# A hybrid attention / RWKV step on one core: per-head means in one fp32 product, key and query loads over 128 partitions, RWKV's room released in two steps

## The chip, the cores and the metric

The kernel runs on one core of one Trainium2 chip. The metric is the device time of one launch in microseconds (us); lower is better. The kernel before took 2118.08, 2123.41 and 2121.22 us in three runs, a median of 2121.22. The profile is of one more execution, of 2118.56 us, whose span (first to last instruction) is 2116.8 us at a mean granted TensorE clock of 0.98.

## The reference

One step of a two-layer model over 256 context and 1024 latent tokens of width 1024. Layer 0 projects the normed input to attention queries, keys, values and gates and to the operands of a bidirectional RWKV scan, runs both, gates each branch, and projects back. Layer 1 does the same with a chunked gated linear attention (GLA). Cut to what the change touches:

```python
z = h @ w_in
qa, ka, va, ga, zb, gb = split_cols(z, EV_SPLITS)
q = rms_norm(qa.reshape(B, T, H_A, HD_A), qn_g)   # a mean of squares over the 64 columns of each head
k = rms_norm(ka.reshape(B, T, KV_A, HD_A), kn_g)
...                                               # RWKV: kk is normalised per head too
o_a = block_attention(q, keys, vals) * jax.nn.silu(ga)      # 8 query heads, 2 key heads, 64 wide, fp32
```

## The kernel before, in words

**Who sets the order.** The kernel is written as generators that hand every operation to a list scheduler (class `Sched`, L86 on). It estimates a start and a cost for each operation, keeps a time for every engine, and issues the one that can start first; where an operation may go to several engines, `_best` (L271) takes the cheapest by start + cost + a fee of the engine (`WORTH`, L112). So a changed fee or cost moves instructions anywhere in the program. The resulting order on TensorE (PE), VectorE (DVE), ScalarE (ACT) and GpSimd (POOL) is fixed when the kernel is built: each engine runs its list in order and stalls at the first instruction whose input is missing. Transfers are issued by SP, also in order. Each takes one of eight semaphores in turn (DMAHW0 to 7) and is not issued until the transfer eight before it, on the same semaphore, has ended. All recorded instructions carry the line number of the issuing helper (L354), so the profile is read by tile names.

**Layer 0's projections (0 to 525 us).** Weights and activations are split in high and low parts (`hhi`, `hlo`, `whi`, `wlo`; type fp32r), and each product of a projection is three fp32r products (`mm3`), 8 k-slices deep: 24 rows of PE per 128 columns and 512 tokens. Results land in the PSUM tiles `pj`. Queries, keys and RWKV's kk need a mean of squares per head. `head_means` (L965) gets it as a product with the 128x128 block matrix `bones`: it splits the squares into `hi` (a cast) and `lo` (a subtraction) and adds two fp32r products in a PSUM tile `a`.

**The changeover (about 515 to 560 us).** When the projections have let go of their memory, `room_attn` (L1187) lays out attention's tiles and `room_rwkv` (L1248) RWKV's. Keys come from `kh` in DRAM: `KA` holds the high part of a key head in rows 0 to 63 and the low part in rows 64 to 127, `KB` the high part again in rows 0 to 63 and a row of ones (row 64). A query tile `QA` holds the high part of a head's queries twice, `QB` the low part and, in row 64, the negated row maximum `mr`. Loads of `KA` and `QA` are two transfers of 64 partitions each. `maxima` (L1615) makes one product KA,QA per 128 queries and 512 keys and reduces it on DVE (`mx`); `attend` (L1648) then makes the score pair KA,QA and KB,QB, an exponential (`pt`) and the product with the values `VO`. `mod_cols` (L548) computes modulation columns from the weights `mw`.

**RWKV beside attention (560 to 1240 us).** Four head pairs run a chunked scan of small products (`AR`, `BK`, `Vs` are loaded per segment; `Z`, `TT`, `U` and others are its tiles); `rwkv_norm` (L1562) normalises `y` with fp32 products with `bones`. Attention fills in between, in 12 units with two heads each.

**After it.** `room_proj` (L2211) closes RWKV's memory and starts to load layer 0's output weights; the output projection runs at about 1310 to 1450 us, layer 1 to about 1990, its output projection to the end.

Of the kernel before, what the change touches and what calls it, by code (L numbers as in the profile page):

```python
# [20 lines left out]
P = 128  # L21
# [82 lines left out]
class Sched:  # L104
# [4 lines left out]

    OWN = {"dve": 0.085, "act": 0.085}  # L110
    SWITCH = 0.095
    WORTH = {"dve": 0.2, "act": 0.0, "pool": 0.6}  # L112
    AFTER = {"pe": 0.07, "": -0.13}
    UNTIL = {"pe": 0.26, "pool": 0.19, "dve": 0.13, "act": 0.13}

# [60 lines left out]
    def _instr(self, name, op, f, a, k):  # L176
# [19 lines left out]
        if name == "pe":  # L196
            lhs = pattern(k.get("lhsT", a[1] if len(a) > 1 else None))
            m = 1
            for d in lhs.shape[1:]:
                m *= d  # L200
            rows = lhs.shape[0]
            turned = op == "transpose" or k.get("is_transpose")

            if turned:
                cost = max(2 * n / 2300, m / 1170)
            elif lhs.dtype == F32:
                cost = 2 * max(2 * n / 2300, m / 1170)
            elif lhs.dtype == F32R:
                cost = max(n / 2300, m / 1170)
            else:  # L210
                cost = max(n, 64) / 2300
            cost = 1.06 * cost + 0.0025
            size = lambda x: 32 if x <= 32 else 64 if x <= 64 else P
            late = (size(rows), size(m), lhs.start_partition() // 32, out.start_partition() // 32)
        elif name == "dve":
            srcs = [x for _, x in aps if x is not out]
            psum = any(x.tensor.space == PSUM for x in [out] + srcs)
            if op == "reduce_max":
                n = 1
# [12 lines left out]
            late = not psum and op != "reduce_max"  # L232
            if op in ("tensor_scalar", "scalar_tensor_tensor"):
                cost += (0.0, 0.057, 0.09)[sum(1 for x in srcs if x.shape[1:] == [1] or tuple(x.shape[1:]) == (1,))] if n > 1 else 0.0
        elif name == "act":
            psum = any(x.tensor.space == PSUM for _, x in aps)
            cost = (0.051 if psum else 0.094) + n * 0.833e-3
            if n > 1:
                cost += (0.0, 0.05, 0.17)[min(2, sum(1 for q, x in aps if q in ("scale", "bias", 2)))]
            if out.shape[0] <= 64 and n > 1:  # L240
                cost += 0.11
        elif name == "pool":
            if op == "tensor_tensor":
                cost = 0.15 + n * (1.66e-3 if any(0 == d[0] for _, x in aps for d in x.ap[1:]) else 2.1e-3)
                if k.get("op", a[-1]) == ALU.pow:
                    cost = 0.56
            elif op == "memset":
                cost = 0.14 + n * 0.42e-3
            else:
                cost = 0.16 + n * (0.833e-3 if len(aps) == 2 else 1.5e-3)  # L250
            late = op != "memset"
        else:
            cost, late = 0.47, n * out.shape[0] * 4 / 270e3
        return f, a, k, name, cost, late, reads, writes, slots

    def _choice(self, slot, taken=()):
# [14 lines left out]
    def _best(self, ins):  # L271

        if len(ins) == 9:
            return ins
        ts = [(self._start(x), x) for x in ins[9]]
        if ts[0][0] is None:
            return ins[9][0]
        return min(ts, key=lambda x: x[0] + x[1][4] + self.WORTH.get(x[1][3], 0.0)
                   + (self._beside(x[1][3], x[0], x[1][4]) if x[1][3] in self.port and x[1][5] else 0.0))[1]

    def _start(self, ins, spare=0.0):
# [202 lines left out]
def tile_hybrid_dit_step(ctx: ExitStack, tc: tile.TileContext, I, C, O):  # L484
# [63 lines left out]
    def mod_cols(i, c0, n, bank, row, ready=lambda: True):  # L548
# [15 lines left out]
                b = yield from get(row, False)  # L564
                D.dma_start(out=b[0:2, 0:n], in_=I["mod_b"][i:i + 1, c0:c0 + n].to_broadcast([2, n]))
        yield from sch.until(ready)
        for a in range(2):
            with sch.together():
                for s in range(4):
                    k = 4 * a + s  # L570
                    PE.matmul(p[32 * s:32 * s + 32, :], lhsT=sT[:, k, :], rhs=ws[k // nk][:, k % nk, :], start=(a == 0), stop=(a == 1))
            for x in ws[4 * a // nk:4 * (a + 1) // nk]:
                put("mw", x)
        m4 = yield from get("m4", False)
        m = m4[:, 0:n]
        copy(m, p)
# [123 lines left out]
    vt_d = [dram.tile([T, P], F32, name=f"vt{p}") for p in range(4)]  # L700
    bv_d = [dram.tile([P, T], F32, name=f"bv{p}") for p in range(4)]
    kh_d = dram.tile([P, 2, PAST + T], F32, name="kh")
    vo_d = dram.tile([P, 14, P], F32, name="vo")
    ga_d = [dram.tile([P, T], F32, name=f"ga{p}") for p in range(4)]
    gb_d = [dram.tile([P, T], F32, name=f"gb{p}") for p in range(4)]
# [6 lines left out]

    get, put = sch.get, sch.put
    el = cst.tile([P, 2, 4, 20], F32, name="el")
    left, right = (ctx.enter_context(ExitStack()) for i in range(2))
    flags = dict(left=0, gates=0, attn=False, keys=False, rwkv=False, mods=False, normed=False, gla=False, gl=False, units=0)

    def pool(stack, name, **k):
        return stack.enter_context(tc.tile_pool(name=name, bufs=1, reuse_waits="tile", **k))
# [18 lines left out]
    def layer0():  # L738
# [44 lines left out]

        def gated(col, dst):

            def use(g, t0, n, p):
                t1 = yield from get("gt", False)
                S.activation(out=t1[:, 0:n], in_=p, func=AF.Tanh, scale=0.5)
                V.scalar_tensor_tensor(out=t1[:, 0:n], in0=t1[:, 0:n], scalar=1.0, in1=p, op0=ALU.add, op1=ALU.mult)
# [8 lines left out]
        def gated_unit(i, col, dst):  # L798
            yield from sch.until(lambda: flags["left"] <= GATES[i])
            yield from gated(col, dst)  # L800

            def done():
                flags["gates"] += 1
            sch.then(done)

        def gates():
            for i in range(8):
# [156 lines left out]

        def head_means(p, x, n):  # L965

            hi, lo = yield from parts(x, n)
            PE.matmul(p, lhsT=bones, rhs=hi[:, 0:n], start=True, stop=False)
            PE.matmul(p, lhsT=bones, rhs=lo[:, 0:n], start=False, stop=True)
            put("hi", hi)  # L970
            put("lo", lo)

        def operands(p, g):
            yield from sch.until(lambda: have[p] == 3)
# [212 lines left out]
    def room_attn():  # L1187
# [11 lines left out]
        sT = ac.tile([P, NK, 32], F32, name="sT1")  # L1199
        for x in ("QA", "QB"):  # L1200
            slots(x, 4, [P, 512], F32R)
        slots("mx", 2, [P, 4, 4])
        slots("mr", 1, [4, P], F32R)
        slots("rcp", 1, [P, 512])
# [3 lines left out]
        yield from move("a", "po", 1)  # L1208
        yield from move("a", "b", 3)
        yield from move("pj", "b", 2)  # L1210
        for x in range(2):
            load_keys(0, x)
        for v in range(2):
            V.memset(KB[v][64:65, :].bitcast(F32), 1.0)
        D.dma_start(out=sT.rearrange("p k c -> p (k c)"), in_=sT_d)
        V.memset(ones64, 1.0)

# [3 lines left out]

    def load_keys(v, x):

        D.dma_start(out=(KA, KA, KB)[x][v][64 * (x % 2):64 * (x % 2) + 64, :].bitcast(F32), in_=kh_d[64 * v:64 * v + 64, x % 2, :])

    def keys():

        yield from sch.until(lambda: flags["attn"])
        for v, x in ((0, 2), (1, 0), (1, 1), (1, 2)):
            load_keys(v, x)  # L1230
            if (v, x) == (0, 2):
                D.dma_start(out=VO.rearrange("p t v d -> p t (v d)"), in_=vo_d)

        def done():
            flags["keys"] = True
        sch.then(done)

    def mods():
# [9 lines left out]
    def room_rwkv():  # L1248
# [1 line left out]
        nonlocal gmask, zmask, id16, m116, hm, id2, ring  # L1250
        yield from sch.until(lambda: flags["gates"] == 8 and flags["attn"])
        left.close()
        rc = pool(left, "rc", side="left")
        slots = slots_in(rc)
        yield from move("pj", "b", 4 - 2)
        gmask = rc.tile([P, 2, P], F32, name="gmask")
        D.dma_start(out=gmask, in_=C["k_gmask"].rearrange("p (d c) -> p d c", d=2))
        zmask = rc.tile([P, 2, 5, 64], F32, name="zmask")
        D.dma_start(out=zmask, in_=C["k_zmask"].rearrange("p (d l c) -> p d l c", d=2, l=5))
        slots("gsq", 1, [P, 512])  # L1260
        m1t = yield from get("gsq")
        m1f = m1t[:, 0:2 * P].rearrange("p (d c) -> p d c", d=2)
        D.dma_start(out=m1f, in_=C["k_m1"].rearrange("p (d c) -> p d c", d=2))
# [8 lines left out]
            V.memset(hm[64 * h:64 * h + 64, h:h + 1], 1.0)  # L1272
        id2 = rc.tile([P, 64], F32, name="id2")
        V.tensor_tensor(id2, ident[:, 0:64], ident[:, 64:128], ALU.add)
        slots("y", 2, [P, T])
        slots("AR", 3, [P, 3, 4, 64])
        slots("BK", 3, [P, 2, 4, 64])
        slots("Vs", 3, [P, 2, 2, 64])
# [19 lines left out]
                         fv(id16[:, d * h:d * h + 1], [[0, 4], [2 * h, 64 // h], [1, h]]))  # L1298
        slots("GH", 2, [P, 2, 2 * SEG])
        slots("sm", 2, [P, 64])  # L1300
        slots("rv", 1, [P, T])
        ring = [[rc.tile([P, 64], F32, name=f"ring{h}{i}") for i in range(NRING)] for h in range(4)]
        for q in range(4):
            for i in range(NRING):
# [310 lines left out]
    def maxima(i, p4, g):  # L1615


        yield from sch.until(lambda: flags["attn"] and (p4 < 2 or flags["keys"]))
        t0, n, k0, nk = span(g)
        before = sum(scores(x) for _, x in units[0:i])  # L1620
        kv = p4 // 2
# [3 lines left out]
        for hh, hs in enumerate(halves):  # L1625
            QA = yield from get("QA")
            QB = yield from get("QB")
            for x in range(2):
                D.dma_start(out=QA[64 * x:64 * x + 64, 0:n].bitcast(F32), in_=qh_d[p4][hs, 0, t0:t0 + n])
            D.dma_start(out=QB[0:64, 0:n].bitcast(F32), in_=qh_d[p4][hs, 1, t0:t0 + n])  # L1630
            mx = yield from get("mx")
            for j in range(n // P):
# [22 lines left out]
    def attend(i, p4, g):  # L1655
# [11 lines left out]
        for kt in range(nk + 1):  # L1667
            new = []
            for hh in range(2):
                if kt < nk:  # L1670
# [5 lines left out]
                    p = yield from get("b", False)  # L1676
                    with sch.together():
                        PE.matmul(p[:, 0:n], lhsT=KA[kv][:, kc], rhs=Q[hh][0][:, 0:n], start=True, stop=False)
                        PE.matmul(p[:, 0:n], lhsT=KB[kv][0:65, kc], rhs=Q[hh][1][0:65, 0:n], start=False, stop=True)
                    S.activation(out=pt[:, 0:n], in_=p[:, 0:n], func=AF.Exp, scale=0.125)  # L1680
                    put("b", p)
                    new.append(pt)
# [526 lines left out]
    TILES = [tt for g in ORDER for tt in range(10) if g == (0 if tt < 2 else (tt + 2) // 4)]  # L2209

    def room_proj():  # L2211
        yield from sch.until(lambda: rwkv_over[0] == 4)
        left.close()
        out_pool(0, left, "wo0", 2)
        slots_in(pool(left, "xr", side="left"))("xr", 1, [P, NK, P])
        yield from move("b", "pj", 3)
# [170 lines left out]
```

## Time and profile before

| what | value |
|---|---|
| median of three runs | 2121.22 us |
| profiled execution, its span | 2118.56 us, 2116.8 us |
| PE busy | 1997.0 us (94%) |
| DVE busy | 1456.1 us (69%) |
| ACT busy | 1010.9 us (48%) |
| POOL busy | 324.2 us (15%) |
| mean transfer rate | 104 GB/s |

A group of instructions is named by output and inputs (`a<-hi,bones` is the product of tile hi with bones into PSUM tile a), and buffer numbers are left out. Matmuls overlap one another: the duration of one row is longer than the distance to the next. PEclk is the granted clock of TensorE as a share of its full 2.4 GHz. The share under DMA is the mean busy share of the core's 16 DMA engines. A chain of waits names what ended each idle stretch.

### The profile page before, as it was taken

To read this page: it belongs to the slowest core of one execution; us is meant where nothing else is said; L and a number is where in the kernel's file an instruction comes from. 1 tells how busy PE (TensorE), PEld (TensorE's weight loads), DVE (VectorE), ACT (ScalarE), POOL (GpSimd) and SP (SyncE) were. 2 spreads that over 40 slices of the span, in tenths; PEclk is the share of its full clock that TensorE was granted. 3 is DMA by queue.
4 is the path that set the end of the run, shared out by engine and by line. 5 is a ranking of instruction groups with operands and counts; after the bars stand their busy time and mean duration, and the time that the engine had idled before them with its cause. 6 is when DMAs were issued, how large, how long until landed. Compare 5 with 4: busy or idle time off the path is not lost.

```text
span 2116.8 us, 38599 instructions
## 1 busy us (share of the span) xinstructions
PE 1997.0 (94%) x14876; PEld 1556.8 (74%) x14876; DVE 1456.1 (69%) x2852; ACT 1010.9 (48%) x2196; POOL 324.2 (15%) x392
## 2 busy tenths in 40 slices
PE   5999989999799999999999998999999999999998
PEld 3787777786477777777777754777777777778886
DVE  4578776767787888879887876643565656564455
ACT  4355554552466666665666543342445454542111
POOL 2011211102311111121112012110121212110011
PEclk7999999999899999999999999999999999999999
DMA  8234353526612241233222224442111111105653
GB/s 284 70 100 157 105 177 103 176 80 217 189 50 76 76 128 59 86 93 102 68 89 85 71 75 145 152 134 73 34 33 43 34 43 33 43 26 162 192 168 115
DMA packets 218264, 219.57 MB, mean 104 GB/s; under 512 B 20624, under 2 KB 164352, under 8 KB 218080
## 3 DMA queue, kind: packets, MB, share of 16 engines
q1 hardware_dynamic: 218080, 217.10, 32.6%
q8 instruction: 117, 1.92, 0.4%
q14 instruction: 67, 0.55, 0.1%
HBM read 149.63 MB, written 67.39 MB: 103 GB/s over the span
## 4 chain that ended last, share of the span: by engine, by line
PE 55%; DVE 11%; issue 3%; ACT 3%; DMA 2%; POOL 1%; SPq 0%; POOLq 0%; DVEq 0%; ACTq 0%
PE pj L354 28%; PE a L354 27%; DVE QQ L354 2%; DVE mx L354 1%; DVE dec L354 1%; ACT QQ L354 1%; DVE LL L354 1%; DVE gt L354 1%; DMA gb<-gt 1%; DMA x<-xt 1%; DVE acc L354 1%; DVE TT L354 1%; DVE Z L354 1%; POOL wol L354 0%; DMA wst<-o 0%
## 5 line engine op out<-in xcount | busy, mean ns | idle before, releaser
L354 PE MATMUL pj<-hhi,whi 128*128 128x512 f32 (+1 forms) x672 | 240.8, 360 | 5.6 <-DVE whi L354 2.9
L354 PE MATMUL pj<-hlo,whi 128*128 128x512 f32 (+1 forms) x672 | 241.0, 360 | 1.0 <-DVE hlo L354 1.0
L354 PE MATMUL pj<-hhi,wlo 128*128 128x512 f32 (+1 forms) x672 | 239.4, 360 | 2.2 <-DVE wlo L354 2.2
L354 PEld LDWEIGHTS pj<-hhi,whi 128*128 128x128 f32 x672 | 128.4, 191 | 29.0 <-issue 6.3
L354 PEld LDWEIGHTS pj<-hlo,whi 128*128 128x128 f32 x672 | 128.4, 192 | 24.8 <-issue 5.6
L354 PEld LDWEIGHTS pj<-hhi,wlo 128*128 128x128 f32 x672 | 128.2, 191 | 24.9 <-issue 4.2
L354 POOL TENSOR_TENSOR acc<-acc,pt 128x512 f32<-128x512 f32 (+1 forms) x57 | 75.8, 1337 | 457.1 <-ACT pt L354 325.7
L354 PE MATMUL a<-h1hi,whi 128*128 128x512 f32 (+3 forms) x304 | 111.1, 368 | 1.7 <-ACT whi L354 1.7
L354 PE MATMUL a<-h1lo,whi 128*128 128x512 f32 (+3 forms) x304 | 110.9, 366 | 0.0
L354 PE MATMUL pj<-h1lo,whi 128*128 128x512 f32 (+2 forms) x296 | 109.5, 370 | 1.3 <-DVE h1lo L354 1.3
L354 PE MATMUL pj<-h1hi,whi 128*128 128x512 f32 (+2 forms) x296 | 110.0, 372 | 0.0
L354 PE MATMUL pj<-h1hi,wlo 128*128 128x512 f32 (+1 forms) x288 | 107.2, 372 | 0.0
L354 PE MATMUL a<-h1hi,wlo 128*128 128x512 f32 (+1 forms) x288 | 105.5, 366 | 0.0
L354 PE MATMUL a<-pt,VO 128*64 128x512 f32 (+1 forms) x368 | 96.6, 604 | 1.2 <-ACT pt L354 1.2
L354 DVE TENSOR_TENSOR acc<-acc,pt 128x512 f32<-128x512 f32 (+1 forms) x127 | 89.0, 724 | 11.1 <-ACT pt L354 8.7
L354 POOL TENSOR_SCALAR sq<-sq 128x1 f32<-128x1 f32 x70 | 18.7, 267 | 442.0 <-ACT gt L354 157.7
L354 DVE TENSOR_REDUCE mx<-pj 128x1 f32<-128x512 f32 (+1 forms) x122 | 78.4, 655 | 5.6 <-PE pj L354 5.6
L354 ACT ACTIVATE pt<-pj 128x512 f32<-128x512 f32 (+1 forms) x103 | 58.6, 592 | 26.3 <-PE pj L354 18.0
L354 DVE TENSOR_REDUCE mx<-a 128x1 f32<-128x512 f32 (+1 forms) x86 | 56.6, 669 | 14.9 <-PE a L354 14.9
L354 PE MATMUL pj<-woh,oh 128*128 128x512 f32 (+1 forms) x160 | 61.1, 382 | 5.0 <-DVE oh L354 5.0
L354 PEld LDWEIGHTS a<-h1hi,whi 128*128 128x128 f32 (+1 forms) x304 | 56.5, 186 | 11.1 <-ACT whi L354 1.9
L354 PEld LDWEIGHTS pj<-h1lo,whi 128*128 128x128 f32 (+1 forms) x296 | 56.3, 190 | 10.5 <-DVE h1lo L354 1.7
(505 smaller groups left out, 5519.2 us busy)
## 6 DMA issues: line engine op xcount, KB each, us to landing
mw<-in_mod_w SPq DMA_DIRECT2D x24, 1024.0 KB
ws<-wk SPq DMA_DIRECT2D x32, 512.0 KB
wst<-in_ev_w_in SPq DMA_DIRECT2D x26, 512.0 KB
wst<-in_od_w_in SPq DMA_DIRECT2D x24, 512.0 KB
AR<-ws SPq DMA_DIRECT2D x40, 256.0 KB
BK<-ws SPq DMA_DIRECT2D x40, 256.0 KB
wst<-o SPq DMA_DIRECT2D x14, 512.0 KB
Vs<-vt SPq DMA_DIRECT2D x80, 64.0 KB
```

The source lines that it names most:

```text
L354: r = f(*a, **k)
```

## The change

The head means become one product of fp32 operands, without hi and lo. KA and QA are loaded by one transfer each, whose source is described by `twice`: an outer dimension of 2 (the high and low part for KA, the same data twice for QA, by a stride of 0), then 64 rows, then the columns. The zero rows that QB and KB then need are set by POOL, and the second score product runs over all 128 rows. The second key head is loaded later in the program, gates count as done earlier, `mod_cols` makes its 256-column products in one group, POOL's fee falls from 0.6 to 0.3 while its costs count 1.5 times, transfers of at most 64 partitions are reckoned at 180 GB/s, and RWKV's memory is let go in two steps: the segments' tiles when all scans are over, the norm's later.

```diff
-    WORTH = {"dve": 0.2, "act": 0.0, "pool": 0.6}
+    WORTH = {"dve": 0.2, "act": 0.0, "pool": 0.3}
+    HOLD = 0.5
...
-            cost, late = 0.47, n * out.shape[0] * 4 / 270e3
+            parts = [x.shape[0] for _, x in aps if x.tensor.space != DRAM]
+            cost, late = 0.47, n * out.shape[0] * 4 / (270e3 if not parts or parts[0] > 64 else 180e3)
...
-        return min(ts, key=lambda x: x[0] + x[1][4] + self.WORTH.get(x[1][3], 0.0)
+        return min(ts, key=lambda x: x[0] + x[1][4] * (1 + self.HOLD * (x[1][3] == "pool")) + self.WORTH.get(x[1][3], 0.0)
...
+    twice = lambda x, r, c, s: bass.AP(tensor=x.tensor, offset=x.offset, ap=[[s, 2], [x.ap[0][0], r], [1, c]])
...
         def head_means(p, x, n):
-            hi, lo = yield from parts(x, n)
-            PE.matmul(p, lhsT=bones, rhs=hi[:, 0:n], start=True, stop=False)
-            PE.matmul(p, lhsT=bones, rhs=lo[:, 0:n], start=False, stop=True)
-            put("hi", hi)
-            put("lo", lo)
+            PE.matmul(p, lhsT=bones.bitcast(F32), rhs=x, start=True, stop=True)
+            yield
...
+        for x in [t.bitcast(F32) for t in sch.slot["QB"]]:
+            G.memset(x[64:128], 0.0)
...
-            V.memset(KB[v][64:65, :].bitcast(F32), 1.0)
+            G.memset(KB[v][64:128, :].bitcast(F32), 0.0)
+            G.memset(KB[v][64:65, :].bitcast(F32), 1.0)
...
-        D.dma_start(out=(KA, KA, KB)[x][v][64 * (x % 2):64 * (x % 2) + 64, :].bitcast(F32), in_=kh_d[64 * v:64 * v + 64, x % 2, :])
+        src = kh_d[64 * v:64 * v + 64, 0, :]
+        if x == 0:
+            D.dma_start(out=KA[v].bitcast(F32), in_=twice(src, 64, PAST + T, PAST + T))
+        else:
+            D.dma_start(out=KB[v][0:64, :].bitcast(F32), in_=src)
...
+        yield from sch.until(lambda: attended[1] >= 2)
+        for x in range(2):
+            load_keys(1, x)
...
-        rc = pool(left, "rc", side="left")
+        rn = pool(right, "rn", side="right")
+        rc = pool(segs, "rc", side="left")
...
-            for x in range(2):
-                D.dma_start(out=QA[64 * x:64 * x + 64, 0:n].bitcast(F32), in_=qh_d[p4][hs, 0, t0:t0 + n])
+            D.dma_start(out=QA[:, 0:n].bitcast(F32), in_=twice(qh_d[p4][hs, 0, t0:t0 + n], 64, n, 0))
...
-                        PE.matmul(p[:, 0:n], lhsT=KB[kv][0:65, kc], rhs=Q[hh][1][0:65, 0:n], start=False, stop=True)
+                        PE.matmul(p[:, 0:n], lhsT=KB[kv][:, kc], rhs=Q[hh][1][:, 0:n], start=False, stop=True)
...
     def room_proj():
-        yield from sch.until(lambda: rwkv_over[0] == 4)
-        left.close()
+        yield from sch.until(lambda: all(x["over"] == 10 for x in sts))
+        segs.close()
```

The order of SP's transfers at the changeover, before; KA0 and KA1 are the two key heads, QA_0 the first query tile, kh and qh0 the DRAM tensors:

```order
L354 DMA KA0_3798<-kh_91 64x1792 [waits DMAHW0_49,PE_49]
L354 DMA KA0_3798<-kh_91 64x1792 [waits DMAHW1_49]
L354 DMA sT1_3806<-sT_d_66 128x256 [waits DMAHW2_49]
L354 DMA QA_0_3807<-qh0_101 64x512 [waits DMAHW3_49]
L354 DMA QA_0_3807<-qh0_101 64x512 [waits DMAHW4_49]
L354 DMA QB_0_3811<-qh0_101 64x512 [waits DMAHW5_49,PE_49]
L354 DMA KB0_3800<-kh_91 64x1792 [waits DMAHW6_49,Pool_49]
L354 DMA VO_3802<-vo_92 128x1792 [waits DMAHW7_49]
L354 DMA KA1_3799<-kh_91 64x1792 [waits DMAHW0_49]
```

and now, the same place and the one of KA1 some rows further on (AR is RWKV's first operand):

```order
L357 DMA KA0_3626<-kh_91 128x1x1792 [waits DMAHW6_49,PE_49]
L357 DMA sT1_3634<-sT_d_66 128x256 [waits DMAHW7_49]
L357 DMA QA_0_3635<-qh0_101 128x1x512 [waits DMAHW0_49]
...
L357 DMA QA_1_3636<-qh0_101 128x1x512 [waits DMAHW6_49]
...
L357 DMA KA1_3627<-kh_91 128x1x1792 [waits DMAHW2_49]
...
L357 DMA gb3_100<-gt_1_133 128x512 [waits DMAHW2_49,DVE_49]
L357 DMA AR_0_3887<-ws00_75 128x512 [waits DMAHW3_49]
```

Two transfers became one, KA1's moved behind the first query tiles, and the transfer gb3 just ahead of AR_0 waits for KA1's (semaphore 2).

TensorE's order where the first scores begin, before (the three products of a projection, then the scores of the first query tile, the modulation products, the next query tile, and RWKV's first product):

```order
L354 MATMUL pj_1_141<-hhi_151,wlo_1_157 128x512
L354 MATMUL a_2_146<-KA0_3798,QA_0_3807 128x512 [waits DMAHW3_49,DMAHW4_49,DMAHW1_49,DMAHW0_49]
...
L354 MATMUL pj_0_140<-ident_60,mx_0_3815 4x128 [waits DVE_49]
L354 MATMUL a_3_147<-mw_0_3804,sT1_3806 32x256 [waits DMAHW4_49,DMAHW2_49]
...
L354 MATMUL a_1_145<-KA0_3798,QA_1_3808 128x512 [waits DMAHW7_49,DMAHW6_49]
...
L354 MATMUL pj_1_141<-AR_0_3973,BK_0_3976 128x128 [waits DMAHW2_49,DMAHW1_49]
```

and now:

```order
L357 MATMUL pj_1_141<-hhi_151,wlo_2_158 128x256
L357 MATMUL pj_0_140<-KA0_3626,QA_0_3635 128x512 [waits DMAHW6_49,DMAHW0_49]
...
L357 MATMUL pj_3_143<-ident_60,mx_0_3643 4x128 [waits DVE_49]
L357 MATMUL a_3_147<-mw_0_3632,sT1_3634 32x256 [waits DMAHW7_49,DMAHW4_49]
...
L357 MATMUL pj_2_142<-hhi_151,whi_2_155 128x512 [waits DVE_49]
...
L357 MATMUL a_0_144<-KA0_3626,QA_1_3636 128x512 [waits DMAHW6_49]
...
L357 MATMUL pj_1_141<-hhi_151,whi_2_155 128x512 [waits DVE_49]
```

Two projection groups of 24 products, which stood ahead of the first scores, now stand behind the first and inside the second query tile's. The first scores stand behind three other groups (24 products of 512, 24 of 512, 24 of 256 columns) that follow the last head mean.

## Rows read from the trace of the kernel before

**Rows 1.** The page: busy time and share of the span by engine.
```profile
PE 1997.0 (94%) x14876; PEld 1556.8 (74%) x14876; DVE 1456.1 (69%) x2852; ACT 1010.9 (48%) x2196; POOL 324.2 (15%) x392
```
**Rows 2.** Windows: from:to, length, busy us (count) per engine, clock, DMA share, GB/s.
```profile
150.00:200.00 50.00, 44.95 (x220) 35.08 (x219) 45.45 (x71) 28.73 (x47) 8.41 (x5) 0.97 0.56 187
525.00:560.00 35.00, 19.95 (x109) 10.97 (x108) 22.94 (x51) 10.13 (x27) 15.87 (x31) 0.76 0.85 242
1300.00:1350.00 50.00, 39.80 (x214) 32.33 (x215) 23.40 (x36) 8.73 (x21) 7.74 (x6) 0.93 0.40 127
```
**Rows 3.** Waits of PE, 100 to 500 us: total us, times, longest.
```profile
PE a L354 <- ACT hi L354: 11.9, 7, 3.1
PE a L354 <- POOL lo L354: 2.7, 3, 1.1
PE a L354 <- DVE lo L354: 2.7, 3, 1.7
PE a L354 <- DVE hi L354: 2.6, 1, 2.6
```
**Rows 4.** Instructions by tile bones: ns least/median/most, first and last start.
```profile
L354 PE MATMUL a<-hi,bones x39: 278/393/508, 107.2 to 510.6; 128*128 128x512 f32 x26, 128*128 128x256 f32 x13
L354 PE MATMUL a<-lo,bones x39: 279/393/776, 107.6 to 511.3; 128*128 128x512 f32 x26, 128*128 128x256 f32 x13
L354 PE MATMUL a<-y,bones x12: 377/592/676, 737.8 to 1242.1; 128*128 128x512 f32 x8, 128*128 128x256 f32 x4
```
**Rows 5.** Timeline of PE at 740 us: start, us, instruction, merged count.
```profile
740.37 1.02 PE L354 MATMUL a<-y,bones 128*128 128x512 f32 x2
```
**Rows 6.** Instructions by tile hi, 100 to 500 us (columns as in rows 4).
```profile
L354 DVE TENSOR_TENSOR lo<-t,hi x22: 411/684/693, 105.7 to 445.7; 128x512 fp32r<-128x512 f32 x15, 128x256 fp32r<-128x256 f32 x7
L354 ACT CAST hi<-t x22: 404/620/622, 143.4 to 444.0; 128x512 fp32r<-128x512 f32 x15, 128x256 fp32r<-128x256 f32 x7
```
**Rows 7.** Waits of PE, 500 to 560 us.
```profile
PE a L354 <- DMA gb<-gt: 6.8, 1, 6.8
PE pj L354 <- DVE mx L354: 5.5, 3, 2.7
```
**Rows 8.** Timeline of PE at the first scores.
```profile
526.01 0.47 PE L354 MATMUL a<-KA,QA 128*128 128x512 f32 x1 [0.54 <-DMA QA<-qh]
526.32 0.62 PE L354 MATMUL pj<-KA,QA 128*128 128x512 f32 x2
```
**Rows 9.** Timeline of SP, 510 to 556 us: start and us of each issue.
```profile
515.92 2.23 SPq L354 DMA_DIRECT2D KA<-kh  x2
```
**Rows 10.** Transfers of 1200 to 1204 us: packets, issues.
```profile
DMA packets 8, 0.00 MB, mean 1 GB/s; under 512 B 4, under 2 KB 8, under 8 KB 8
...
gate<-m SPq DMA_DIRECT2D x1, 2.0 KB
gt<-in_mod_b SPq DMA_DIRECT2D x1, 2.0 KB
```
**Rows 11.** Transfers of 716 to 721 us: 40 slices of GB/s, packets, share of 16 engines, issues.
```profile
GB/s 344 328 328 361 295 311 344 360 279 82 33 98 229 197 246 213 98 148 213 213 361 148 213 115 262 262 99 16 16 0 0 0 33 98 82 197 377 197 180 131
DMA packets 553, 0.94 MB, mean 188 GB/s; under 512 B 95, under 2 KB 95, under 8 KB 553
...
q1 hardware_dynamic: 553, 0.94, 63.6%
```
**Rows 12.** Issues on SP of two query tiles in RWKV's stretch.
```profile
716.14 1.11 SPq L354 DMA_DIRECT2D QA<-qh  x2
...
953.52 1.10 SPq L354 DMA_DIRECT2D QA<-qh  x2
```
**Rows 13.** The first score products of these two tiles on PE.
```profile
722.81 0.71 PE L354 MATMUL pj<-KA,QA 128*128 128x512 f32 x2
...
958.25 0.48 PE L354 MATMUL a<-KA,QA 128*128 128x512 f32 x1
```
**Rows 14.** Waits of PE, 1240 to 1500 us.
```profile
PE a L354 <- DVE oh L354: 6.3, 1, 6.3
```

More of the change, by code (lines that the diff above doesn't have):

```diff
@@ L566, in mod_cols @@
         yield from sch.until(ready)
-        for a in range(2):
+        for ks in [range(NK)] if nk == NK else (range(4), range(4, NK)):
             with sch.together():
[L569 to L573, printed above, removed]
+                for k in ks:
+                    PE.matmul(p[32 * (k % 4):32 * (k % 4) + 32, :], lhsT=sT[:, k, :], rhs=ws[k // nk][:, k % nk, :],
+                              start=(k < 4), stop=(k >= 4))
+            put("mw", ws[ks[0] // nk])
         m4 = yield from get("m4", False)
@@ L714, in tile_hybrid_dit_step @@
     el = cst.tile([P, 2, 4, 20], F32, name="el")
-    left, right = (ctx.enter_context(ExitStack()) for i in range(2))
-    flags = dict(left=0, gates=0, attn=False, keys=False, rwkv=False, mods=False, normed=False, gla=False, gl=False, units=0)
+    left, segs, right = (ctx.enter_context(ExitStack()) for i in range(3))
+    flags = dict(left=0, gates=0, attn=False, keys=0, rwkv=False, mods=False, normed=False, gla=False, gl=False, units=0)
     def pool(stack, name, **k):
@@ L784, in gated, with done @@
         def gated(col, dst):
+            def done():
+                flags["gates"] += 1
             def use(g, t0, n, p):
+                if g == 2:
+                    sch.then(done)
                 t1 = yield from get("gt", False)
@@ L800, in gated_unit @@
             yield from gated(col, dst)
-            def done():
-                flags["gates"] += 1
-            sch.then(done)
         def gates():
@@ L1210, in room_attn @@
         yield from move("pj", "b", 2)
-        for x in range(2):
-            load_keys(0, x)
+        load_keys(0, 0)
         for v in range(2):
-            V.memset(KB[v][64:65, :].bitcast(F32), 1.0)
+            G.memset(KB[v][64:128, :].bitcast(F32), 0.0)
+            G.memset(KB[v][64:65, :].bitcast(F32), 1.0)
         D.dma_start(out=sT.rearrange("p k c -> p (k c)"), in_=sT_d)
@@ L1222, in load_keys @@
     def load_keys(v, x):
-        D.dma_start(out=(KA, KA, KB)[x][v][64 * (x % 2):64 * (x % 2) + 64, :].bitcast(F32), in_=kh_d[64 * v:64 * v + 64, x % 2, :])
+        src = kh_d[64 * v:64 * v + 64, 0, :]
[3 more added lines that the diff above has]
+            D.dma_start(out=KB[v][0:64, :].bitcast(F32), in_=src)
     def keys():
         yield from sch.until(lambda: flags["attn"])
[L1229 to L1232, printed above, removed]
         def done():
-            flags["keys"] = True
+            flags["keys"] += 1
+        load_keys(0, 1)
+        D.dma_start(out=VO.rearrange("p t v d -> p t (v d)"), in_=vo_d)
+        sch.then(done)
+        yield from sch.until(lambda: attended[1] >= 2)
+        for x in range(2):
+            load_keys(1, x)
         sch.then(done)
@@ L1259, in room_rwkv @@
         D.dma_start(out=zmask, in_=C["k_zmask"].rearrange("p (d l c) -> p d l c", d=2, l=5))
-        slots("gsq", 1, [P, 512])
+        slots("gsq", 1, [P, 512], pool=rn)
         m1t = yield from get("gsq")
@@ L1274, in room_rwkv @@
         V.tensor_tensor(id2, ident[:, 0:64], ident[:, 64:128], ALU.add)
-        slots("y", 2, [P, T])
+        slots("y", 2, [P, T], pool=rn)
         slots("AR", 3, [P, 3, 4, 64])
@@ L1300, in room_rwkv @@
         slots("sm", 2, [P, 64])
-        slots("rv", 1, [P, T])
+        slots("rv", 1, [P, T], pool=rn)
         ring = [[rc.tile([P, 64], F32, name=f"ring{h}{i}") for i in range(NRING)] for h in range(4)]
@@ L1615, in maxima @@
     def maxima(i, p4, g):
-        yield from sch.until(lambda: flags["attn"] and (p4 < 2 or flags["keys"]))
+        yield from sch.until(lambda: flags["attn"] and (p4 < 2 or flags["keys"] == 2))
         t0, n, k0, nk = span(g)
@@ L1627, in maxima @@
             QB = yield from get("QB")
-            for x in range(2):
-                D.dma_start(out=QA[64 * x:64 * x + 64, 0:n].bitcast(F32), in_=qh_d[p4][hs, 0, t0:t0 + n])
+            D.dma_start(out=QA[:, 0:n].bitcast(F32), in_=twice(qh_d[p4][hs, 0, t0:t0 + n], 64, n, 0))
             D.dma_start(out=QB[0:64, 0:n].bitcast(F32), in_=qh_d[p4][hs, 1, t0:t0 + n])
```

## The prediction

> **What bounds the kernel now.** I read the page's busy shares first: TensorE is busy for 94% of the span and no other engine for more than 69% [rows 1], so time is lost or won as PE work that is added or removed and as idle of PE, and the idle there is only some 120 us. The windows show where it lies. In layer 0's projections PE idles 5.05 us of 50 at 150 to 200 us, with DVE busy for 45.45 [rows 2]: the two run nearly level there. Over the changeover, 525 to 560 us, PE is busy 19.95 of 35 us at a mean clock of 0.76, while the DMA engines are 85% busy [rows 2]: 15 us idle, and some 4 to 5 of the busy ones stand at the lower clock. Around 1300 to 1350 us another 10.2 us are idle [rows 2]. The waits then name who holds PE: from 100 to 500 us the casts and subtractions ahead of the head means, 11.9 + 2.7 + 2.7 + 2.6 = 19.9 us [rows 3]; at the changeover a DMA (6.8 us) and the reductions of the scores (5.5) [rows 7].
>
> **Head means.** There are 39 of them, 26 of 512 columns and 13 of 256 [rows 4]. A pair of fp32r products costs twice the distance of two such products: two rows of 512 columns take 0.62 us and one takes 0.39, so 0.23 each, 0.46 a pair [rows 8, 4]. An fp32 product of 512 columns is two rows of 592 ns that together take 1.02 us, so 0.43 each, 0.86 [rows 4, 5]. The difference is 0.40, and half for 256 columns: 26 x 0.40 + 13 x 0.20 = 13 us more on PE. Removed are a cast and a subtraction each, 0.62 and 0.68 us one behind the other [rows 6]. PE's 19.9 us of waits named after them do not all go: the new product still waits for what made the squares (on ACT or DVE, one step up), and DVE, 91% busy there, loses some 22 subtractions of squares x 0.68 = 15 us [rows 6] and as many again for keys and queries, out of 400 us, so it still runs above 80%. Bounds: none or all of the 19.9 returned, so +13 to -7. I take 12 returned, which is +1.
>
> **Changeover without the transfers' new form.** Two groups of 24 products, 48 x 0.23 = 11 us, come from ahead of the first scores to between them. There PE waited for reductions and for a DMA [rows 7], 12.3 us. Of these I take 5 us as filled, bounds 0 and 12: -5. The memsets that POOL takes over (QB 4 x 512 columns, KB 2 x 1792 twice) come when it is already 15.87 of 35 us busy [rows 2]; RWKV's own first products come at its end, so they are hidden, and at worst push them by their length, some 8 us, estimated by columns.
>
> **Release in two steps, and the rest.** Output weights load before RWKV's last norm and no longer after it. PE's waits there are 6.3 us for DVE's `oh` [rows 14] in a stretch with 10.2 idle [rows 2]. I take -6, bounds -10 and +3 (the last attention's chain may end as late as before). Fees that move five sums and five weight splits from POOL to DVE fall mostly into layer 1, where DVE has room: 0. The second score product over 128 rows instead of 65 streams as many columns: 0. The sum so far is +1 - 5 - 6 = -10.
>
> **The transfers, which decide.** From 1200 to 1204 us two transfers of two rows of 1 KB each left 8 packets: 4 of data and 4 under 512 B [rows 10]. I read the small ones as the word by which each DMA engine that took part reports its end: two engines each. From 716 to 721 us six transfers of 64 rows and the start of a seventh left 95 words, near 16 each [rows 11]. So the rows of the outer dimension, up to 16, set the number of engines. Now KA and QA come by `twice`, and their source has an outer dimension of 2. If that counts, each runs on two engines.
>
> The Trainium skill states this as a rule (DMA: Bandwidth & Descriptors, Why a DMA increments its semaphore by 16 and not by 1, and Rules for kernel authors): the engines are the largest number up to 16 that divides the slowest dimension of both sides, and a leading zero-stride broadcast of c copies keeps a transfer on at most c engines. The counts of rows 10 and 11 agree with it; no transfer of before has 2 on one side and 128 on the other. The same page advises one transfer of 128 partitions over two on disjoint halves, which alone would make this edit worth its saved issues.
>
> The price. KA is 917 KB, so 459 KB on each of two engines; QA is 262 KB, so 131 KB. A single engine's rate: 0.94 MB in 63.6% of 16 x 5 us is 18.5 GB/s, and the best slice, 377 GB/s over 16, is 23.6 [rows 11]. KA thus takes 19.5 to 25 us and QA 5.6 to 7.1, against about 3 and 1 before. I take the quick ends, as the other 14 engines are idle or nearly so.
> - First scores. KA is issued 4.6 us after the last head mean (511.3 to 515.92) [rows 4, 9]. In the new order 24 + 24 groups of 512 columns and 24 of 256 follow that mean, 48 x 0.23 + 24 x 0.12 = 14 us, so PE asks for the scores 9.4 us after the issue. KA and the QA queued behind it on the same two engines need 19.5 + 5.6 + about 1 = 26. PE idles 16.6 us; only products that stand behind the scores in order are left, and these can't start.
> - KA1 is issued once QA_2 has landed, about 37 us after KA0's issue, and lands with QA_3 in front about 25 us later. The gb transfer just ahead of AR_0 waits for KA1's semaphore, and so do RWKV's first operands and the row maxima `mr` of the second query tile. Between the first scores and the use of that tile PE has some 33 us of work, so it comes 59 us after KA0's issue, and the maxima about 67. I take 10 us, bounds 0 and 20.
> - The other 20 query tiles. From issue to first product are 6.7 us at one and 4.7 at the other [rows 12, 13], where 5.6 + 2 are needed and the second head's tile queues behind the first. At 1 to 3 us for most of ten units I take 14, bounds 4 and 25.
>
> Together 16.6 + 10 + 14 = 40.6 and -10: 31 us above the profiled execution's 2118.6, so 2149. The median of the runs lies 2.7 us above that execution, so 2151; I say 2150.
>
> **Rivals.** (1) The transfers still use 16 engines, since SP or the compiler cuts them by the 128 rows of the target. Then the sum is -10: 2109, or 2111 on the runs' scale, with 2098 to 2122 by the bounds; fewer issues of SP speak for nothing more, since SP is not waited for. This ends faster. It decides where 16 words follow each KA. (2) Two engines, but with loads early enough: if KA0's room comes free 10 us earlier in relation to the scores and the query tiles are issued earlier than in rows 12 and 13 (four buffers would allow it), 40 shrinks to about 10 and cancels the -10: 2120. Against it stands that KA waits for memory that only the projections' end sets free. (3) Sixteen engines, but head means that return nothing: +13, and the changeover and the end bring 0: 2134. DVE's 45.45 of 50 us [rows 2] speaks for it, as the squares themselves then come late.
>
> **How the numbers follow.** Forecast 0.53, rival 1 0.22, rival 2 0.14, rival 3 0.11. By the bounds the forecast's own range is 2122 to 2182. To hold 8 in 10 the range reaches into rival 1: 2106 to 2182. A change within 0.3%, 6.4 us, can't be told from none. Faster: nearly all of rival 1 and a little of 2, 0.22. Same: most of rival 2, a little of the others, 0.13. Slower: the rest, 0.65.
>
> **What would show it.** Two small packets behind each KA and QA transfer, and long stretches with some 45 GB/s; PE idle before the first KA,QA product for more than 10 us, named DMA, with the clock down behind it; a second DMA wait ahead of QB or AR; waits on QA in RWKV's stretch. Head means: y-like rows of 592 ns at 100 to 511 us and waits on `t`, `qr` and `kd` of some 8 us in place of 19.9. If KA's bytes move at over 200 GB/s, the forecast is wrong and rival 1 holds; if PE's waits on DMA at the changeover are long but the total is not, the products that moved there covered more than I reckon.

## The result, and the profile after

The changed kernel took 2172.81 us (median of four runs, 2166.56 to 2177.79) against 2121.27 for the kernel before; the ratio is 1.0243, interval 1.021 to 1.0275. It is slower by 2.4%, inside the stated range of 2106 to 2182 and 23 us above the 2150 forecast. Its profiled execution spans 2173.8 us, 57 us more than before. The page's busy line, which answers to [rows 1], shows 25 us more of busy PE, so some 32 us of the 57 are idle. Not all of the 25 us is added work. Run 1 below executes the same products, and its page has 17.5 us less for them (second line), at a mean clock of 0.985 against 0.969 here:

```profile
PE 2022.2 (93%) x14876; PEld 1564.4 (72%) x14876; DVE 1437.6 (66%) x2830; ACT 994.2 (46%) x2156; POOL 287.6 (13%) x386
```
```profile
PE 2004.7 (95%) x14876; PEld 1552.7 (74%) x14876; DVE 1442.3 (69%) x2830; ACT 993.2 (47%) x2156; POOL 290.8 (14%) x386
```

The windows of the changeover (from:to, length, busy us and count of PE, PEld, DVE, ACT, POOL, then clock, DMA share, GB/s) answer to the second row of [rows 2]. The first two are of the changed kernel, the third is the kernel before in the 40 us that follow:

```profile
525.00:560.00 35.00, 18.35 (x62) 11.08 (x62) 10.34 (x19) 1.50 (x4) 0.00 (x0) 0.66 0.56 156
560.00:600.00 40.00, 16.39 (x73) 9.59 (x74) 10.54 (x30) 7.66 (x21) 12.88 (x26) 0.61 0.44 145
```
```profile
560.00:600.00 40.00, 39.73 (x439) 29.27 (x437) 34.56 (x81) 25.42 (x59) 10.94 (x13) 1.00 0.33 98
```

Before, the trouble ended at 560 us. Now it lasts to 600, at a clock of 0.61 and with the DMA engines only half busy. PE's waits from 490 to 620 us (in all, times, longest) name two long ones, which answer to [rows 7]:

```profile
PE pj L357 <- DVE gt L357: 21.2, 2, 18.6
PE pj L357 <- DMA QA<-qh: 20.9, 1, 20.9
```

**The first scores.** SP's timeline (start, us of the issue) and PE's first score product:

```profile
505.84 0.62 SPq L357 DMA_DIRECT2D KA<-kh  x1
506.50 0.51 SPq L357 DMA_DIRECT2D sT<-sT_d  x1
507.07 0.52 SPq L357 DMA_DIRECT2D QA<-qh  x1
507.63 15.68 SPq L357 DMA_DIRECT2D QB<-qh  x1
```
```profile
535.64 0.79 PE L357 MATMUL pj<-KA,QA 128*128 128x512 f32 x1 [20.88 <-DMA QA<-qh]
```

KA is issued 10 us earlier than in [rows 9], PE asks for it 9 us later and waits 20.9. While KA is under way the transfers of 506 to 524 us (40 slices of GB/s, then share of the 16 engines) go at a crawl, against 188 GB/s in [rows 11]:

```profile
GB/s 321 388 141 34 205 32 48 64 48 48 64 48 48 64 48 64 48 48 64 48 48 64 48 64 48 48 64 48 48 64 48 48 64 48 48 64 48 48 64 48
DMA packets 610, 1.32 MB, mean 73 GB/s; under 512 B 48, under 2 KB 365, under 8 KB 610
...
q1 hardware_dynamic: 610, 1.32, 20.3%
```

From 510 to 523 us nothing but KA moves:

```profile
DMA packets 97, 0.70 MB, mean 53 GB/s; under 512 B 0, under 2 KB 0, under 8 KB 97
...
q1 hardware_dynamic: 97, 0.70, 12.7%
```

12.7% of 16 engines is 2.03: two engines, busy all the time, at 53 GB/s together. SP itself is held too: the issue of QB, behind KA, sT and QA, takes 15.68 us.

**The second stall** came by a road that I had not seen. ACT writes a gate tile `gt`, which SP stores to `gb`; there are two `gt` tiles:

```profile
556.88 0.52 SPq L357 DMA_DIRECT2D KA<-kh  x1
560.21 1.88 SPq L357 DMA_DIRECT2D gb<-gt  x1
...
585.71 0.32 SPq L357 DMA_DIRECT2D gb<-gt  x1
```
```profile
584.37 0.60 ACT L357 ACTIVATE gt<-pj 128x512 f32<-128x512 f32 x1 [24.64 <-DMA gb<-gt]
```

The store of 560.21 runs on all engines, so two of its parts queue behind KA1 (556.88). The packets of the trace show it: 112 of the store's 128 rows of 1 KB start by 563.04 us, the last 16 only from 583.40 on. ACT gets its tile back at 584.37, DVE reads the PSUM tile after it, and PE's next group waits 18.6 us for that:

```profile
585.74 1.93 PE L357 MATMUL pj<-mw,sT 128*32 128x256 f32 x16 [18.61 <-DVE gt L357]
```

**In RWKV's stretch**, 620 to 1300 us, waits on query tiles stand where the kernel before has none (its slack is in [rows 12, 13]):

```profile
PE a L357 <- DMA QA<-qh: 5.9, 2, 3.8
PE pj L357 <- DMA QA<-qh: 2.7, 1, 2.7
```

**Head means.** Their rows have the durations that [rows 4] gave for y (592 ns), and the waits ahead of them from 100 to 500 us fell from 19.9 [rows 3] to about 10:

```profile
PE a L357 <- DVE kd L357: 8.4, 7, 3.6
PE a L357 <- ACT t L357: 1.3, 1, 1.3
```
```profile
L357 PE MATMUL a<-t,bones x54: 377/591/697, 107.9 to 436.4; 128*128 128x512 f32 x36, 128*128 128x256 f32 x18
```

### The profile page after: what moved, and what is told of

Its sections match the earlier page's. It is cut to its first block, busy times and chain, and to the rows that moved or that the text cites. A ratio compares the mean times of both kernels' runs of the same rounds, so it can differ in the third digit from the quotient of the medians.

```text
span 2173.8 us, 38473 instructions
## 1 busy us (share of the span) xinstructions
PE 2022.2 (93%) x14876; PEld 1564.4 (72%) x14876; DVE 1437.6 (66%) x2830; ACT 994.2 (46%) x2156; POOL 287.6 (13%) x386
## 4 chain that ended last, share of the span: by engine, by line
PE 66%; DVE 16%; DMA 8%; issue 5%; ACT 4%; POOL 1%; SPq 0%; DVEq 0%; POOLq 0%; ACTq 0%
PE pj L357 37%; PE a L357 29%; DMA QA<-qh 2%; DVE wk L357 2%; DMA gb<-gt 2%; DVE QQ L357 2%; DVE mx L357 1%; DVE sgta L357 1%; DMA QB<-mr 1%; DVE kd L357 1%; ACT QQ L357 1%; DVE gt L357 1%; DMA mw<-in_mod_w 1%; DVE TT L357 1%; DVE LL L357 1%
## 5 line engine op out<-in xcount | busy, mean ns | idle before, releaser
L357 PE MATMUL pj<-hhi,whi 128*128 128x512 f32 (+1 forms) x672 | 247.3, 370 | 8.2 <-DVE whi L357 2.9
L357 PEld LDWEIGHTS pj<-hlo,whi 128*128 128x128 f32 x672 | 128.8, 192 | 23.6 <-issue 5.7
L357 POOL TENSOR_TENSOR acc<-acc,pt 128x512 f32<-128x512 f32 (+1 forms) x52 | 66.9, 1294 | 370.8 <-ACT pt L357 236.5
L357 PE MATMUL a<-h1lo,whi 128*128 128x512 f32 (+3 forms) x296 | 106.5, 361 | 0.0
L357 PE MATMUL a<-woh,oh 128*128 128x512 f32 (+1 forms) x184 | 69.2, 376 | 9.6 <-DVE oh L357 9.6
L357 PE MATMUL pj<-KA,QA 128*128 128x512 f32 (+1 forms) x118 | 51.2, 457 | 24.6 <-DMA QA<-qh 23.5
L357 PE MATMUL a<-woh,ol 128*128 128x512 f32 (+1 forms) x184 | 69.0, 375 | 0.8 <-DVE ol L357 0.8
L357 ACT ACTIVATE pt<-pj 128x512 f32<-128x512 f32 (+1 forms) x108 | 61.2, 590 | 17.5 <-PE pj L357 15.1
L357 PE MATMUL a<-wol,oh 128*128 128x512 f32 (+1 forms) x184 | 68.8, 374 | 0.0
```

What stands on the lines that cost most here:

```text
L357: r = f(*a, **k)
```

## The experiments

Times are medians; ratios are to the kernel before, run on the same chip beside them. A table of starts (us) stands at the end of the section. In runs 1 to 4 the compute engines keep the order of the kernel that was edited. In runs 5 to 10 the scheduler makes a new order, so such a run measures its edit together with that order.

**1. Rows outermost.** Only the order of the source's dimensions:

```diff
-    twice = lambda x, r, c, s: bass.AP(..., ap=[[s, 2], [x.ap[0][0], r], [1, c]])
+    twice = lambda x, r, c, s: bass.AP(..., ap=[[x.ap[0][0], r], [s, 2], [1, c]])
```

> The changed kernel, with the source of KA and QA described with the 64 rows outermost and the two copies inside (partitions then hold high and low of a row next to each other in both tiles, so the products are the same sums). Every engine's order stays as in the changed kernel. Theory A (two DMA engines carry each such load): the KA and QA loads run on all engines, PE's waits of 20.9 us before the first scores and of 18.6 us on gt vanish, and the time falls to 2105 to 2120. Rival B (the new order itself costs it: RWKV starts late because attention and two projection groups stand ahead of it): the first AR product stays more than 30 us later than before and the time stays above 2140. Rival C (the outer dimension does not set the engines): no change, 2173.

Measured: 2108.23 us, 0.9935 (0.9921 to 0.995), as theory A had it. The same instructions in the same order on PE, DVE, ACT and POOL are now faster than the kernel before; the two engines cost 1.0243 - 0.9935 = 3.1%, 65 us. PE's scores follow the projections without a wait:

```profile
512.91 0.28 PE L357 MATMUL pj<-hhi,wlo 128*128 128x256 f32 x1
513.03 0.39 PE L357 MATMUL pj<-KA,QA 128*128 128x512 f32 x1
```

Rival B falls, since the first AR product is 8.9 us later than before and not over 30; rival C falls.

**2 and 3. KA alone, QA alone in two transfers.** Cut at issue, so that the compute engines' order stays the changed kernel's; for KA (abridged):

```diff
-        r = f(*a, **k)
+        i = k.get("in_")
+        if name == "sync" and list(i.ap[0])[1] == 2 and i.ap[2][1] == 1792:   # QA: <= 512
+            for h in range(2):
+                r = f(out=k["out"][64 * h:64 * h + 64], in_=half(i, h))
+        else:
+            r = f(*a, **k)
```

> The changed kernel, with only KA's two loads cut in two transfers of 64 rows each when they are issued; QA stays one transfer with an outer dimension of 2, and the order of the compute engines is untouched. Theory A: the 20.9 us fall to below 8 (QA alone), the 18.6 us on gt vanish, QA's waits in RWKV's stretch stay near 9 us: 2122 to 2138. Rival B: above 2145. If the query tiles were the main cost instead: above 2155.

> The changed kernel, with only QA's loads cut in two transfers of 64 rows each when they are issued; KA stays one transfer with an outer dimension of 2, and the order of the compute engines is untouched. Theory A: the waits of 20.9 and 18.6 us stay at above 14 each (KA alone takes 17 us), the QA waits of 9 us in RWKV's stretch vanish: 2152 to 2166. If the query tiles were the main cost: below 2140.

Measured: 2145.75 us (1.0106, 1.0088 to 1.0124) with KA cut, 2142.52 (1.0092, 1.0075 to 1.0108) with QA cut. Both miss their ranges, the first to the slow and the second to the fast side: the query tiles cost more than I had reckoned, and KA alone less. The first also lies above the 2145 that I had set for rival B; run 1, in the same order, rules that rival out. With QA still on two engines, 500 to 620 us show

```profile
PE pj L362 <- DMA QA<-qh: 7.2, 1, 7.2
PE pj L362 <- DVE gt L362: 6.1, 1, 6.1
```

and with KA still on two

```profile
PE a L362 <- DVE mx L362: 19.0, 1, 19.0
PE pj L362 <- DMA QA<-qh: 18.1, 1, 18.1
```

The wait on `gt`, which I had expected to vanish with KA cut, keeps 6.1 us. With QA cut it bears the name of `mx`, but it is the same stall: the reduction stands behind `gt` in DVE's order, and ACT waits for the store of `gt`:

```profile
578.25 0.60 ACT L362 ACTIVATE gt<-pj 128x512 f32<-128x512 f32 x1 [16.97 <-DMA gb<-gt]
```

Against run 1, KA alone adds 1.0092 - 0.9935 = 33 us, QA alone 1.0106 - 0.9935 = 36, both together 65. The table shows where QA's lie: RWKV's products take 681 us from first to last with QA on two engines, 660 without. Waits that name QA are only 8.6 us of these 21; the rest lies in smaller stalls and, in the changed kernel, in windows with the clock at 0.94 to 0.97, which I did not take apart.

**4. The merged loads in the old order.** The kernel before, its pairs of 64-row loads issued as one transfer with the outer dimension 2; PE's and DVE's order is that of before. The edit, abridged:

```diff
-        r = f(*a, **k)
+        if <64 rows of KA or QA>:
+            first half: keep it; second half: r = f(out=<128 rows>, in_=AP([[s, 2], [row, 64], [1, c]]))
+        else:
+            r = f(*a, **k)
```

> The kernel before, in its own order on every compute engine, with each pair of 64-row loads of KA and of QA issued as the one transfer of the change (outer dimension 2). Theory A: the two-engine loads alone cost here what they cost in the changed kernel, 45 to 75 us, by waits on KA and QA at the first scores and on QA between 560 and 1250 us: 2166 to 2196. Rival B (only the new order is sensitive to them, since before had the projections ahead of the scores): below 2140.

Measured: 2188.23 us, 1.0303 (1.0287 to 1.0319), again 3.0%. So the price is no matter of the new order. Here it shows as (500 to 620 us)

```profile
PE a L367 <- DMA QA<-qh: 23.2, 2, 19.5
PE a L367 <- DMA mw<-in_mod_w: 20.4, 1, 20.4
```

The second wait is on weights that have 128 rows; they were issued at 546.75, behind KA1 (538.02).

**5. Only the fp32 head means**, on the kernel before (the diff is that of `head_means` above).

> The kernel before with the head means as one fp32 product and nothing else of the change. PE gains 13 us of work; the waits on hi and lo (19.9 us) go, others on the squares come. Forecast: +1, so 2118 to 2126. If the fp32 work is hardly returned: 2127 to 2135. If the freed DVE and ACT pay for it and more: below 2117.

Measured: 2147.34 us, 1.011 (1.0091 to 1.0128), 24 us slower: above all that I had named. PE waited from the end of attention to the first output product:

```profile
1309.89 0.98 PE L354 MATMUL pj<-acc,ones 128*64 128x256 f32 x4
1340.56 0.55 PE L354 MATMUL pj<-woh,oh 128*128 128x256 f32 x1 [29.69 <-DVE oh L354]
```

RWKV starts 19 us later and ends 30 later, and from its last norm to the first output product pass about 60 us (1279.1 to 1340.6 here, 1249.0 to 1309.6 before). Before, attention's tail filled them to the end; now it runs out at 1310.

Where the 19 us at RWKV's start come from is seen in the order. With the fp32 means the scheduler puts the first scores ahead of two projection groups:

```profile
516.93 0.47 PE L354 MATMUL pj<-KA,QA 128*128 128x512 f32 x1 [1.66 <-DMA QA<-qh]
```
```profile
544.52 0.40 PE L354 MATMUL pj<-hhi,wlo 128*128 128x512 f32 x1
```

So it is in every run with the fp32 means (last projection product and first score at 539.0 and 513.0 us in run 1, 537.4 and 511.6 in run 8). In every run with the old ones the projections end first (525.1 and 526.0 before, 514.9 and 517.7 in run 6, 516.3 and 521.5 in run 9). These are the two groups of the change's own order. Had they stayed ahead, their 48 x 0.23 = 11 us [rows 8] would put the first scores of this run at an estimated 528, 2 us later than before (6 by the same working for run 1 against run 6). By that estimate the fp32 products alone cost 2 to 6 us, and most of the 24 us goes with the new order; no run parts the two.

**6. Rows outermost and the old head means**: run 1 with `head_means` as before.

> As the first of these runs, with the head means again as high and low part (two fp32r products each, with the casts and subtractions). The scheduler's order follows. Theory A with the forecast's +1 us for the head means: within 6 us of the first of these runs. If the fp32 product's 13 us are not returned by the casts that go: 8 to 15 us faster than it. If the casts were worth more than that: slower than it by 5 or more.

Measured: 2103.28 us, 0.9913 (0.9896 to 0.993), 5 us faster than run 1: within the forecast's 6, and with intervals that overlap. RWKV's first product comes at 540.3 us, 22 earlier than in run 1, and its last 26.5 earlier; by the first output product that lead is as large (26.4), and by the first of layer 1 it is down to 9.

**7. The same with the old release**: run 6 with one pool, and `room_proj` again after RWKV's last norm (`rwkv_over[0] == 4`, `left.close()`).

> As the run with the rows outermost and the old head means, with RWKV's memory let go in one step again and the output weights loaded after the last norm. Forecast's -6 for the release: 2106 to 2112. If the release is worth nothing: 2100 to 2106.

Measured: 2091.3 us, 0.9849 (0.9832 to 0.9866). This is faster than both of my ranges: the release in two steps, which I had put at -6, costs 14 us here. By tile, the output products of run 6 and its last value products (least/median/most ns, first and last start):

```profile
L357 PE MATMUL a<-woh,oh x152: 278/389/776, 1284.8 to 2088.6; 128*128 128x512 f32 x112, 128*128 128x256 f32 x40
...
L357 PE MATMUL a<-pt,VO x368: 379/592/1112, 563.7 to 1326.5; 128*64 128x512 f32 x176, 128*64 128x256 f32 x8
```

The output products start at 1284.8, but attention, from which they take PE, ends at 1326.5; with the old release it ends at 1294.5 and they start at 1294.8. What run 6 loses by it shows from 1330 to 1380 us, where PE is busy 41 us in run 6 (first line) and 49 in run 7:

```profile
1330.00:1380.00 50.00, 41.15 (x175) 33.31 (x176) 25.87 (x37) 19.89 (x45) 3.08 (x6) 0.86 0.40 130
```
```profile
1330.00:1380.00 50.00, 49.10 (x234) 40.72 (x233) 28.99 (x41) 21.54 (x49) 4.54 (x10) 1.00 0.51 158
```

**8. The fp32 means with the old release**: run 1 with the old release, to see whether the two interact.

> The changed kernel with the rows outermost (2108.2) and RWKV's memory let go in one step again, so the fp32 head means meet the old release. Theory A (they interact: the fp32 means let RWKV start and end later, and then the some 60 us from RWKV's last norm to the first output product are no longer covered by attention's tail): PE waits more than 15 us for oh before the first output product, 2118 to 2135. Theory B (both effects simply add, as with the old means, where the old release was 12 us faster): 2093 to 2100.

Measured: 2112.45 us, 0.9952 (0.9939 to 0.9966). Neither range held it, but adding up is refuted: with the old release the fp32 means cost 0.9952 - 0.9849 = 22 us, with the new one 5; the new release costs 14 us with the old means and, if anything, gains 4 with the fp32 ones (0.9935 against 0.9952, intervals overlapping). PE's wait for `oh` (1230 to 1500 us) is there, shorter than I had said:

```profile
PE pj L357 <- DVE oh L357: 11.8, 2, 9.9
```

**9. Only the scheduler's fee and factor for POOL**, on the kernel before (`WORTH`, `HOLD` and `_best` as in the change).

> The kernel before with only the scheduler's fee and factor for POOL changed. In the run with the rows outermost layer 1 became 15 us shorter than before, which the forecast put at 0. If the fees do that (fewer long operations on POOL, whose results layer 1 waits for): layer 1 shorter by 10 to 16 us and 2105 to 2113 in all. If something else of the change does it: layer 1 within 4 us of before, 2116 to 2126.

Measured: 2094.94 us, 0.9865 (0.985 to 0.988): 28 us faster (23 between the profiled executions), more than the best case I had written down. Layer 1 is shorter by 12 us as expected there (564 in place of 576 by the table); as much again comes ahead of it. In layer 1, weight splits on POOL (2385 ns each) went from seven to one:

```profile
L354 POOL TENSOR_TENSOR wlo<-wst,whi x7: 2372/2385/2530, 1542.4 to 1862.5; 128x1024 fp32r<-128x1024 f32 x7
```
```profile
L355 POOL TENSOR_TENSOR wlo<-wst,whi x1: 2388/2388/2388, 1532.6 to 1532.6; 128x1024 fp32r<-128x1024 f32 x1
```

and PE's waits for `QQ` fell from 13.6 to 3.9 us. That `QQ` came late because of these splits is argued from the two counts; no run shows it. From 100 to 500 us the waits for hi and lo fell to half of [rows 3], with the old head means:

```profile
PE a L355 <- ACT hi L355: 4.1, 4, 2.8
PE a L355 <- DVE lo L355: 4.0, 4, 1.4
```

**10. The fees and one load each with the rows outermost**, on the kernel before.

> The kernel before with the changed fee and factor for POOL (2094.9 alone) and KA and QA each in one transfer with the 64 rows outermost. If one transfer in place of two is worth something of its own (fewer issues, earlier landing): 2085 to 2091. If not: 2092 to 2098.

Measured: 2099.06 us, 0.9889 (0.9874 to 0.9904), no better than run 9 and 1 us above what I had expected of a load that is worth nothing. One transfer for two is worth nothing here, even on all engines.

Starts in the profiled executions, us (first AR: RWKV's first product; last AR and last norm: its end; layer 1: its first and last product with `h1hi`):

```
                              first AR  last AR  last norm  first output  layer 1 first  last
before                          553.5   1201.6    1249.0      1309.6        1415.3      1991.1
changed                         607.8   1286.5    1338.7      1377.0        1485.5      2048.9
1 rows outermost                562.4   1222.2    1274.4      1311.2        1419.5      1980.6
2 keys split                    576.5   1257.7    1310.0      1348.5        1456.6      2019.5
3 queries split                 596.9   1256.6    1308.8      1345.4        1453.5      2015.6
5 before, fp32 means            572.7   1230.4    1279.1      1340.6        1448.8      2022.3
6 rows outermost, old means     540.3   1195.7    1242.1      1284.8        1410.3      1971.9
7 the same, old release         540.2   1195.7    1240.5      1294.8        1398.3      1962.2
9 before, fees                  548.7   1195.4    1242.6      1300.9        1403.8      1968.1
```

The version to keep is run 7: the change with the rows outermost, the old head means and the old release, 1.5% faster than the kernel before. Run 9 alone has most of that, and their intervals overlap.

## Why the prediction was right, point by point

- **Two engines decide.** Shown: 2.03 engines busy while KA is under way, and run 1, which turns two dimensions round, moves no compute instruction and takes back 65 us. The count of small packets [rows 10, 11] was enough to see it. The Trainium skill's rule (DMA: Bandwidth & Descriptors, Rules for kernel authors) that a leading broadcast of c copies keeps a transfer on at most c engines agrees, for QA's stride of 0 as for KA's real one. The Trainium skill's advice on the same page, one transfer instead of two on disjoint halves, brought no gain here (run 10).
- **Its price was undersized**, 40.6 us for 65. First scores: 16.6 forecast; they start 535.6 - 513.0 = 22.6 us later than in run 1. PE asked 9 us after the issue, as worked out, but KA and QA landed at about 29 us and not 26. By the packets of the trace KA's last rows start some 19.5 us after its issue, as reckoned; QA's 2 KB rows then run from 526.5 to 534.6 us, 8 us for the 5.6 reckoned, while the other engines carry KB, VO and mw. Second stall: 10 forecast; the first AR product is 607.8 - 562.4 = 45.4 us later than in run 1, so 22.8 beyond the first stall. I had looked at AR_0 and the row maxima; the stall came by the store of `gt`, whose parts queue behind KA1. RWKV's stretch: 14 forecast, 19 measured (678.7 against 659.8 us). The three make 64 of the 65 us. Only the first came as worked out; the second, the most mis-sized, came by another transfer, and in the third the waits that name QA are only 8.6 us.
- **The rest, -10, came out by luck, by errors that cancel.** Run 1 spans 2105.5 us, -11.3. But the terms were wrong: step by step the runs go -28 (fees, run 9), about -3 (what else is in run 7, intervals overlap), +14 (early release) and +5 (fp32 means). Fees: 0 forecast, 28 us of gain alone (run 9); I had counted which operations move and not asked what would stop waiting. Head means: +1 forecast, with bounds of -7 and +13; with the order that comes with them they cost 24 us on the kernel before and 5 (intervals overlap) in the change's surroundings. I summed PE work against waits in their own stretch and did not ask what order the scheduler makes of them, nor follow the later start of RWKV to its end. Release: -6 forecast, with bounds of -10 and +3; measured 14 us of loss with the old means, about -4 with the new.
- **Changeover without the transfers**: the two projection groups do stand between the scores, and run 1 goes through without the DMA waits; but RWKV's first product comes 8.9 us later than before. The -5 was no term of its own: the groups stand there only in the runs with the fp32 means. With the old means (run 6) they stand ahead of the scores and RWKV's first product comes 13.2 us earlier than before, though its last comes no earlier than with the fees alone (1195.7 and 1195.4 us).
- **Rivals.** 1 and 2 are refuted by runs 1 to 4. Rival 3's head means cost more than its +13 on the kernel before (24 us, run 5) and with the old release (22, run 8 against run 7), but only 5, with overlapping intervals, in the change itself; they are not what decided.
- **The ranges.** They were said to follow from the bounds, and they don't: added up, the bounds give 2113 to 2199 for the forecast (2122 to 2182 stated) and 2092 to 2137 for rival 1 (2098 to 2122 stated). The result lies inside either range of the forecast.

## What to carry to other kernels

Before two transfers are merged, look at the outer dimension of both sides: 128 partitions at the target don't help if the source begins with a 2, and turning two dimensions round can cost nothing. A transfer on few engines delayed stores and loads of 128 rows that were issued behind it (`gb`, `mw`), so look not only at its own reader but at stores whose buffers are wanted back. What a later start costs is decided where its chain ends: here the 60 us from RWKV's last norm to the output product were free only as long as attention's tail covered them, and one edit's worth hung on another: the early release lost 14 us with the old means and nothing that can be told from noise with the fp32 ones. Under a list scheduler an edit of one operation is also a new order: compare the two orders before pricing the operation alone.

## What the runs showed of the hardware

- A transfer on two engines holds SP as well: the issue of QB behind KA and QA took 15.68 us, where the same one took 0.61 with the rows outermost and 1.74 with only KA on two engines (run 3), where the issue of `gsq`, behind KA1, took 14.55.
- Two engines alone run at some 53 GB/s, 26 to 27 each, above the 18.5 to 23.6 that I took from a stretch where all 16 worked. By that KA's 917 KB take an estimated 17 us. QA's 262 KB took 8 us, some 32 GB/s on its two engines, at a time when all 16 worked; that the others' traffic slowed it is argued and not tested.
- A transfer that all engines carry ends with its slowest part: the store of `gt` had 112 of its 128 rows under way by 563.04 us and the last 16 from 583.40 on, and in run 4 PE waited 20.4 us for `mw`, which was issued behind KA1.
